# A recurrence in a two-block stack: 16x16 inversions of two units in one pass over 128 lanes, and the products of decayed queries, of removal keys and of the gate's additive part on GpSimd

## The chip, the cores and the metric

The kernel runs on one core of one Trainium2 chip. The metric is the device time of one execution in microseconds (us). The kernel before takes 2347.31 us, the median of 3 runs (2346.71 to 2354.41).

## What is computed

The kernel computes two transformer blocks of two layers each, one after the other, for 256 tokens of width 1024, and the second one also for 256 context tokens. Nearly all of its arithmetic is large projections. The change lies in one mixer, that of the second block's first layer, which runs an attention and beside it a recurrence over the 512 tokens, once forward and once backward, in 8 heads of 64:

```python
def wkv7_scan(S0, inputs, reverse):
    def step(S, inp):
        r, w, k, v, kk, a = inp
        S = (S * w[:, :, None, :]
             - jnp.einsum('bhvk,bhk->bhv', S, kk)[..., None] * (kk * a)[:, :, None, :]
             + v[..., None] * k[:, :, None, :])
        return S, jnp.einsum('bhvk,bhk->bhv', S, r)
    S, y = lax.scan(step, S0, xs, reverse=reverse)

def rwkv7_readout(y, feat, r_k, gn_w, gn_b):
    yn = ((y - mean) * lax.rsqrt(var + GN_EPS)).reshape(Bsz, T, B_WIDTH_2) * gn_w + gn_b
    bonus = (jnp.sum(r * k * r_k, axis=-1, keepdims=True) * v).reshape(Bsz, T, B_WIDTH_2)
    return ((yn + bonus.astype(jnp.float32)) * g.astype(jnp.float32)).astype(g.dtype)
```

The readout's gate is applied as G = gn_w g and H = (gn_b + bonus) g, so that the output is yn' G + H; H is the gate's additive part. The kernel doesn't step token by token: over a chunk of 64 tokens the recurrence becomes matrix products and the inverse of a triangular 64x64 matrix for each head, which is built from the inverses of its four 16x16 blocks on the diagonal.

## The kernel before, in words

The program is written with pools of named tiles; every engine (TensorE or PE, VectorE or DVE, ScalarE or ACT, GpSimd or POOL, and SyncE or SP, whose queue issues all the transfers that are spoken of here) has its own list of instructions. A scheduler puts the instructions of each engine in order, from the order in which the program issues them and from when their operands are ready, before the run; at run time each engine goes through its list and waits at the first instruction whose operands aren't there. A helper `tt` records the operations of two tensors on DVE (all at L120), `acopy` copies on ScalarE (L223) and `vcopy` on DVE (L226).

The work of the recurrence is cut into 8 **units**: a direction d (0 forward, 1 backward) and a tile t of 128 tokens, that is two chunks of 64. A unit passes these steps:

- **Front** (`rwkv_in` L1453, up to its first `yield`): the decays. sg goes through ScalarE (L1475), eo and ei hold the exponents of the summed decays and of their negatives, ak gets the rates.
- **Back** (the rest of `rwkv_in`): fe is loaded with r, k and kk (L1500; one buffer, so that the load waits for the unit before). DVE multiplies the keys, two products in ak, then the removal keys and the queries with the decays into ar (L1515 and L1516, `ar[:, :, 2]` and `ar[:, :, 1]`), then ak, and last bk, which is written over the first two thirds of fe (L1519). PE makes the matrices of each head (gg and gh, L1531) of ak and ar, DVE masks them into g. The triangular matrices go to dq in DRAM (L1543), for the backward direction after a transposition on DVE (L1541).
- **Solve** (`rwkv_solve` L1559): dl, loaded from dq (L1563), has one 16x16 block on each of 64 lanes: 2 chunks x 8 heads x 4 blocks. For 14 columns DVE makes a product dt and adds it to dl, 28 operations of 14 to 56 elements for each lane; the diagonal is set, and dy goes to DRAM (L1571).
- **Maps** (`rwkv_maps` L1573): the inverses come back as x (L1592), are transposed (L1593), and two rounds of `product` and `update` (32 matmuls m each, L1598) make the 64x64 inverses of them; between, am is built of ar and of v (L1626), and the products of x1 and am (L1640) go into lw; the products of g and lw (L1654) become z, which is stored over g.
- **Steps** (`rwkv_step` L1662): two for each pair of units, the chain of states si (L1672) and the outputs y (L1681) into yac.

`rwkv` (L1272) runs ten rounds: round n has the back of unit n, the front of unit n+2, the solve of unit n and the maps of unit n-2, and after each odd unit's maps two steps. Between the stages `fill` takes pieces of the attention (`gqa`, scores sc at L1010, transposes L1028, outputs po L1056, with K, vv and qS loaded from DRAM). After units 2 and 3 the gates (`gates` L1378: H = v x bonus + gn_b, then times g) and the readouts run as a side stream. Fronts, backs and solves of the first units come earlier, in `even_mixer` (L1078), in a written order with the last projections:

```python
GA = "l0 q0 r0 r1 r2 r3 k0 f0 v0 b0 s0 f1 f2 b1 f3 s1 v1 v2 v3"
```

(f, b and s are front, back and solve of a unit; v0 to v3 are the four blocks of v, each copied into the one buffer st, L1168, and from there stored to vd, L1170.) Six memsets of lw and si on GpSimd (L1280, L1284) begin `rwkv`; their tiles take the place of tiles of the projections.

Of the kernel before, what the change touches and what calls it, by code (L numbers as in the profile page):

```python
# [12 lines left out]
F32 = mybir.dt.float32  # L13
F32R = mybir.dt.float32r
AF = mybir.ActivationFunctionType
ALU = mybir.AluOpType
# [30 lines left out]
@with_exitstack  # L47
def kernel(ctx: ExitStack, tc: tile.TileContext, A: dict, out: bass.AP, taps=None):
    nc = tc.nc
    V, S, E = nc.vector, nc.scalar, nc.tensor  # L50
    taps = taps or {}

    cpool = ctx.enter_context(tc.tile_pool(name="cpool", bufs=1))
# [4 lines left out]
    def nm(s):  # L58
        uid[0] += 1
        return f"{s}_{uid[0]}"  # L60
# [13 lines left out]
    def pst(tag):  # L74
        pool, n = psum[tag]
        return pool.tile([128, 512], F32, tag=tag, name=nm(tag), bufs=n)
# [6 lines left out]
    def const(name, pool=cpool, tag=None, queue=nc.sync):  # L83
        src = A[name]
        t = pool.tile(list(src.shape), F32, tag=tag or name, name=nm(name))
        queue.dma_start(out=t, in_=src)
        return t
# [31 lines left out]
    def tt(o, a, b, op):  # L119
        V.tensor_tensor(out=o, in0=a, in1=b, op=op)  # L120
# [24 lines left out]
    def bc(ap, n):  # L145
        return ap.unsqueeze(2).to_broadcast([ap.shape[0], ap.shape[1], n])
# [931 lines left out]
    def even_mixer(l, en):  # L1078
        T = 512
        close_psum()  # L1080
        with tc.tile_pool(name=nm("em"), bufs=1) as pk, tc.tile_pool(name=nm("rf"), bufs=2) as fp, \
# [9 lines left out]
            C = {n: const(n, pk) for n in ("rwkv_wa", "rtri", "gmask", "tmask", "eye2", "sgn")}  # L1091
# [6 lines left out]
            bon = pk.tile([128, 4, 8], F32, tag="bon", name="bon")  # L1098
            order = []
            for i, (t0, t1) in enumerate(((2, 3), (0, 1))):  # L1100
                order += [dict(d=d, t=t, u=u, i=i) for u, (d, t) in enumerate(((0, t0), (1, t1), (0, t1), (1, t0)))]
            dq = [dp.tile([64, 1040], F32, tag=f"dq{n}", name=nm("dq")) for n in range(NS)]
            dy = [dp.tile([64, 1040], F32, tag=f"dy{n}", name=nm("dy")) for n in range(NS)]
# [20 lines left out]
            with tc.tile_pool(name=nm("emn"), bufs=1) as wk:  # L1124
# [4 lines left out]
                for j in range(2):  # L1129
                    z, f = en.tile("fu", 512), en.tile("fg", 512, 2)  # L1130
                    tt(z, pss[j], en.rb, ALU.mult)
                    for v in range(2):
                        c = slice(v * 256, v * 256 + 256)
# [12 lines left out]
            with tc.tile_pool(name=nm("ga"), bufs=1) as ga, tc.tile_pool(name=nm("emw"), bufs=2) as wk:  # L1146
# [72 lines left out]
                def do_r(f):  # L1219
# [21 lines left out]
                    for i, x in enumerate((rf, kf, kk)):  # L1241
                        nc.sync.dma_start(out=D["f"][:, 4 * i + f], in_=x)

                units = [rwkv_in(fp, C, D, un) for un in order]

                def front(u):
# [3 lines left out]
                    order[u].update(next(units[u]))  # L1250

                def solve(u):
                    rwkv_solve(C, order[u])

                def do_v(f):
                    vf = shifted(8 + f)
                    stage(D["v"][:, :, f * 128:(f + 1) * 128], 4, [vf[:, t * 128:(t + 1) * 128] for t in range(4)])

                do = dict(k=do_k, q=do_q, l=do_l, r=do_r, v=do_v, f=front, b=back, s=solve)
                for what, n in GA:  # L1260
                    do[what](n)
# [3 lines left out]
            close_half(0)  # L1265
            open_psum(gg=1, m=2, y=1, sc=1, tr=1)
            rwkv(C, D, order, (front, back, solve), bon, yac)
            for cm in reversed(held):
                cm.__exit__(None, None, None)
# [108 lines left out]
    def gates(D, bon, tm, t):  # L1378
        G, H = tm["G"], tm["H"]
        tok = slice(t % 2 * 128, t % 2 * 128 + 128)  # L1380
        nc.sync.dma_start(out=tm["gl"][:, tok], in_=D["lo"][:, 2, t * 128:(t + 1) * 128])
        nc.sync.dma_start(out=H, in_=D["v"][:, t])
        hg = H.rearrange("p (h d) -> p h d", h=8)
        tt(hg, hg, bc(bon[:, t], 64), ALU.mult)
        tt(H, H, tm["gn"][:, 512:], ALU.add)
        yield
        ps = pst("fr")
        E.matmul(out=ps, lhsT=tm["gl"][:, tok], rhs=tm["g2"], start=True, stop=True)
        tt(G, tm["gn"][:, :512], ps, ALU.mult)
        tt(H, H, ps, ALU.mult)  # L1390
        yield
        if t < 2:
            for i, x in enumerate((G, H)):
                nc.sync.dma_start(out=D["g"][:, 2 * t + i], in_=x)
# [55 lines left out]
    def half(i):  # L1450
        return slice(64 * i, 64 * i + 64)

    def rwkv_in(fp, C, D, un):  # L1453
        d, t, u, dq = (un[n] for n in ("d", "t", "u", "dq"))
# [4 lines left out]
        def w512(tag, shape=(128, 4, 128), pool=fp, bufs=None):  # L1459
            return pool.tile(list(shape), F32, tag=tag, name=nm(tag), **({"bufs": bufs} if bufs else {}))  # L1460
# [26 lines left out]
        inc, exc = eo[:, :, :, 1 - d:65 - d], eo[:, :, :, d:64 + d]  # L1487
# [10 lines left out]
        up, wk = C["up"][un["up"]], C["us"]  # L1498
        fe = w512("fe", (128, 12, 128), wk)
        nc.sync.dma_start(out=fe, in_=D["f"][:, :, tok])  # L1500
        rT, kT, kk = fe[:, 0:4], fe[:, 4:8], fe[:, 8:12]
        def c4(a):
            return a.rearrange("p f (c t) -> p f c t", c=2)

        def by_chunk(a):
            return a.rearrange("p f (c s) t -> p (f c) s t", c=2)
# [4 lines left out]
        ar = w512("ar", (128, 4, 3, 128), up)  # L1511
        for f in range(4):
            for ch in range(2):
                S.activation(out=ar[:, f, 0, ch * 64:ch * 64 + 64], in_=C["eye2"], func=AF.Copy, scale=pc[:, f, ch:ch + 1])
        tt(c4(ar[:, :, 2]), c4(kk), exc, ALU.mult)  # L1515
        tt(c4(ar[:, :, 1]), c4(rT), inc, ALU.mult)  # L1516
        tt(by_chunk(ak), by_chunk(ak), ei.rearrange("p f c t -> p (f c) t").unsqueeze(2).to_broadcast([128, 8, 2, 64]), ALU.mult)
        bk = fe[:, 0:8].rearrange("p n t -> p (n t)").rearrange("p (f a t) -> p f a t", f=4, a=4)
        tt(bk.rearrange("p f (c s) t -> p f c (s t)", c=2), ak.rearrange("p f (c s) t -> p f c (s t)", c=2),  # L1519
# [36 lines left out]
    def lanes_of(x):  # L1556
        return x[:, 0:1024].rearrange("l (r c) -> l r c", r=16)[:, :, 0:16]

    def rwkv_solve(C, un):  # L1559
        wk = C["us"]  # L1560

        y = wk.tile([64, 16, 16], F32, tag="dl", name=nm("dl"), bufs=2)
        nc.sync.dma_start(out=y, in_=lanes_of(un["dq"]))  # L1563
        for c in range(1, 15):
            n = 15 - c
            tmp = wk.tile([64, 64], F32, tag="dt", name=nm("dt"), bufs=2)
            o = tmp[:, :c * n].rearrange("p (a r) -> p a r", a=c)
            tt(o, y[:, 0:c, c].unsqueeze(2).to_broadcast([64, c, n]), y[:, c, c + 1:16].unsqueeze(1).to_broadcast([64, c, n]), ALU.mult)
            tt(y[:, 0:c, c + 1:16], y[:, 0:c, c + 1:16], o, ALU.add)
        V.memset(y.rearrange("p a r -> p (a r)")[:, 0:256:17], 1.0)  # L1570
        nc.sync.dma_start(out=lanes_of(un["dy"]), in_=y)  # L1571

    def rwkv_maps(C, D, un):  # L1573
        d, t, u, dy, ar, g = (un[n] for n in ("d", "t", "u", "dy", "ar", "g"))
# [213 lines left out]
    with tc.tile_pool(name="fin", bufs=1) as wk:  # L1788
# [3 lines left out]
        for k in range(0, 8, 2):  # L1792
            o = en.tile("fo", 512, 4).rearrange("p (k t) -> p k t", k=2)
# [133 lines left out]
def _build(arrays, taps=()):  # L1927
    import concourse.bacc as bacc

    nc = bacc.Bacc("TRN2", target_bir_lowering=False, num_devices=1)  # L1930
    A = {n: nc.dram_tensor(f"in_{n}", a.shape, mybir.dt.from_np(a.dtype), kind="ExternalInput").ap() for n, a in arrays.items()}
    out = nc.dram_tensor("out_0", (128, 8, 256), F32, kind="ExternalOutput").ap()
    tp = {n: (nc.dram_tensor(f"tap_{n}", s, F32, kind="ExternalOutput").ap() if s else None) for n, s in dict(taps).items()}
    with tile.TileContext(nc) as tc:
        kernel(tc, A, out, tp)
    return nc
# [10 lines left out]
```

## Time and profile before

| what | value |
|---|---|
| median of 3 runs | 2347.31 us |
| the profiled execution | 2347.3 us, span 2345.5 us |
| busy PE | 2242.3 us, 96% |
| busy DVE | 1568.0 us, 67% |
| busy ACT | 1072.6 us, 46% |
| busy POOL | 5.6 us, 0% |
| granted PE clock, mean | 0.982 |

The profile is of one execution. The span is the time from the first to the last recorded instruction; busy times are sums over an engine's instructions and overlap between engines. The granted clock is the share of PE's full clock that the chip allowed. In the timelines a bracket tells how long the engine was idle before the instruction and what released it.

### The profile page before, as it was taken

Reading aid. Unit: us, or ns where it says so; the run is one execution under the profiler, and the core shown is the slowest. Engines: PE = TensorE matmul, PEld = TensorE weight load, DVE = VectorE, ACT = ScalarE, POOL = GpSimd, SP = SyncE. Lnnn points to the kernel's source line nnn. Section 1 sums busy time; section 2 is a strip of 40 time slices with the busy share of each in tenths; the row PEclk is TensorE's granted clock in tenths of the full one; section 3 lists DMA queues with packets and bytes.
Section 4 is the critical chain, followed back from the end, with each engine's and each line's share of the span. In section 5 each row is a group of like instructions: output and inputs, shape, how many; then the busy total and the mean of one; then the engine's idle time right before and its main releaser. Section 6 shows DMA issues by size and latency. Waiting matters only on the chain.

```text
span 2345.5 us, 35440 instructions
## 1 busy us (share of the span) xinstructions
PE 2242.3 (96%) x13642; PEld 1835.2 (78%) x13642; DVE 1568.0 (67%) x3074; ACT 1072.6 (46%) x1884; POOL 5.6 (0%) x10
## 2 busy tenths in 40 slices
PE   8999998999999998998888999999999999989998
PEld 6688787777787786776667788787778788768998
DVE  7867778766845677889587777338654334786555
ACT  6756666312224637765545222235322223476444
POOL 0000000000000000000000000000000000000000
PEclk9999999999999999999999999999999999999999
DMA  8556545555623545533264565323543232314553
GB/s 293 175 184 212 173 149 165 194 165 167 198 89 115 157 147 138 123 87 83 76 207 135 181 195 182 103 88 132 189 162 132 87 98 97 99 33 140 182 184 121
DMA packets 161946, 342.02 MB, mean 146 GB/s; under 512 B 48625, under 2 KB 76273, under 8 KB 161649
## 3 DMA queue, kind: packets, MB, share of 16 engines
q1 hardware_dynamic: 161056, 339.15, 45.6%
q8 instruction: 108, 1.77, 0.3%
q10 hardware_dynamic: 720, 0.60, 0.1%
q14 instruction: 62, 0.50, 0.1%
HBM read 321.86 MB, written 17.84 MB: 145 GB/s over the span
## 4 chain that ended last, share of the span: by engine, by line
PE 87%; DVE 7%; ACT 4%; DMA 1%; issue 1%; SPq 0%; DVEq 0%; ACTq 0%
PE mm L115 25%; PE mm L117 24%; PE mm L116 24%; PE m L1598 1%; DVE wlo L98 1%; PE tr L219 1%; PE m L1654 1%; DMA fe<-fd 1%; ACT whi L97 1%; PE wm L331 1%; PE po L1056 1%; PE wm L274 1%; PE gg L1531 1%; PE po L541 1%; DVE xl L129 0%
## 5 line engine op out<-in xcount | busy, mean ns | idle before, releaser
L97 ACT CAST whi<-raw 128x1024 fp32r<-128x1024 f32 (+2 forms) x437 | 437.3, 1002 | 984.6 <-PE mm L116 591.5
L115 PE MATMUL mm<-xh,whi 128*128 128x512 f32 (+1 forms) x1912 | 680.1, 359 | 16.6 <-ACT xh L97 9.5
L117 PE MATMUL mm<-xh,wlo 128*128 128x512 f32 (+1 forms) x1912 | 678.1, 356 | 5.2 <-DVE wlo L98 5.0
L116 PE MATMUL mm<-xl,whi 128*128 128x512 f32 (+1 forms) x1912 | 678.6, 356 | 1.2 <-DVE xl L98 1.1
L98 DVE TENSOR_TENSOR wlo<-raw,whi 128x1024 fp32r<-128x1024 f32 (+2 forms) x437 | 507.6, 1163 | 257.2 <-ACT whi L97 251.2
L115 PEld LDWEIGHTS mm<-xh,whi 128*128 128x128 f32 x1912 | 364.5, 191 | 81.1 <-ACT whi L97 16.1
L117 PEld LDWEIGHTS mm<-xh,wlo 128*128 128x128 f32 x1912 | 364.4, 191 | 58.0 <-DVE wlo L98 7.3
L116 PEld LDWEIGHTS mm<-xl,whi 128*128 128x128 f32 x1912 | 364.8, 191 | 53.8 <-DVE xl L98 4.2
L117 PE MATMUL mm<-hh,wlo 128*128 128x512 f32 (+1 forms) x704 | 260.1, 370 | 0.0
L116 PE MATMUL mm<-hl,whi 128*128 128x512 f32 (+1 forms) x704 | 257.9, 366 | 0.1
L115 PE MATMUL mm<-hh,whi 128*128 128x512 f32 (+1 forms) x704 | 257.0, 366 | 0.0
L129 DVE SCALAR_TENSOR_TENSOR macc<-raw,modc,macc 128x1024 f32<-128x1024 f32 x189 | 234.4, 1279 | 0.5
L129 DVE SCALAR_TENSOR_TENSOR xres<-mm,mod,xres 128x256 f32<-128x256 f32 x216 | 96.3, 480 | 164.2 <-PE mm L117 163.9
L120 DVE TENSOR_TENSOR fg<-mm,fg 128x512 f32<-128x512 f32 (+1 forms) x84 | 52.4, 624 | 161.3 <-PE mm L117 160.6
L115 PEld LDWEIGHTS mm<-hh,whi 128*128 128x128 f32 x704 | 132.1, 188 | 27.6 <-issue 2.5
L116 PEld LDWEIGHTS mm<-hl,whi 128*128 128x128 f32 x704 | 132.4, 188 | 26.1 <-DVE hl L98 0.7
L115 PE MATMUL mm<-whi,xh 128*128 128x512 f32 (+1 forms) x360 | 143.4, 404 | 9.2 <-ACT whi L97 8.5
L117 PEld LDWEIGHTS mm<-hh,wlo 128*128 128x128 f32 x704 | 132.2, 188 | 22.9
L116 PE MATMUL mm<-wlo,xh 128*128 128x512 f32 (+1 forms) x360 | 143.7, 399 | 2.8 <-DVE wlo L98 2.8
L117 PE MATMUL mm<-whi,xl 128*128 128x512 f32 (+1 forms) x360 | 142.2, 397 | 0.0
L115 PEld LDWEIGHTS mm<-whi,xh 128*128 128x128 f32 x360 | 68.5, 191 | 31.3 <-ACT whi L97 9.8
L116 PEld LDWEIGHTS mm<-wlo,xh 128*128 128x128 f32 x360 | 69.0, 192 | 17.3 <-DVE wlo L98 5.3
(402 smaller groups left out, 2524.0 us busy)
## 6 DMA issues: line engine op xcount, KB each, us to landing
raw<-in_ffn_in SPq DMA_DIRECT2D x176, 512.0 KB, 3.5
raw<-in_w_mod SPq DMA_DIRECT2D x144, 512.0 KB, 4.5
raw<-in_ffn_out SPq DMA_DIRECT2D x64, 448.0 KB, 3.3
raw<-in_w_in_even SPq DMA_DIRECT2D x32, 512.0 KB, 4.8
raw<-in_w_in_odd SPq DMA_DIRECT2D x32, 512.0 KB, 3.7
raw<-in_ffn_out SPq DMA_DIRECT2D x32, 512.0 KB, 3.5
raw<-in_w_ple_gate SPq DMA_DIRECT2D x16, 512.0 KB, 3.6
raw<-in_even_r SPq DMA_DIRECT2D x15, 512.0 KB, 3.5
```

The costliest lines, as they stand in the source:

```text
L97: S.copy(out=hi, in_=src)
L98: V.tensor_tensor(out=lo, in0=src, in1=r32(hi), op=ALU.subtract)
L115: E.matmul(out=ps, lhsT=ah, rhs=bh, start=first, stop=False)
L116: E.matmul(out=ps, lhsT=ah, rhs=bl, start=False, stop=False)
L117: E.matmul(out=ps, lhsT=al, rhs=bh, start=False, stop=last)
L120: V.tensor_tensor(out=o, in0=a, in1=b, op=op)
L129: V.scalar_tensor_tensor(out=o, in0=a, scalar=s, in1=b, op0=op0, op1=op1)
L219: E.transpose(ps[:, j * 128:(j + 1) * 128], s, ident)
L274: E.matmul(out=ps[32 * j:32 * j + 32, hf * 256:hf * 256 + 256], lhsT=cz[:, 4 * g + j, 10 - 2 * c:42 - 2 * c], rhs=raw[:, j], start=c == 0 ...
L331: E.matmul(out=ps[32 * j:32 * j + 32], lhsT=mod_1[:, 2 - q:34 - q], rhs=acc[:, v, hf * 512:hf * 512 + 512], start=q == 0, stop=q == 2)
L541: E.matmul(out=po[:, 0:128], lhsT=pt[:, j * 128:(j + 1) * 128], rhs=vt[:, j, c], start=j == 0, stop=j == nk - 1)
L1056: E.matmul(out=po[half(a), 0:256], lhsT=vt[:, j], rhs=pt[:, j, 2 * a:2 * a + 2], start=j == 0, stop=j == nk - 1)
```

## The change

Three edits. `rwkv_solve` takes two units: dl has 128 lanes, unit n-1 on the first 64 and unit n on the others, with two loads and two stores, and the 28 operations work on both at once; `solve(u)` does nothing for an even u, and for an odd one solves u-1 and u together, so that s0 in the written order is empty and s1 is the solve of both. In the backs, the two products into ar are issued by GpSimd in place of DVE. In the gates, the two operations that make H before the matmul (times bon, plus gn_b) are too. Line numbers after L1250 rise by 1, after L1571 by 3.

```diff
@@ even_mixer
                 def solve(u):
-                    rwkv_solve(C, order[u])
+                    if u % 2:
+                        rwkv_solve(C, order[u - 1], order[u])
@@ gates
         hg = H.rearrange("p (h d) -> p h d", h=8)
-        tt(hg, hg, bc(bon[:, t], 64), ALU.mult)
-        tt(H, H, tm["gn"][:, 512:], ALU.add)
+        P.tensor_tensor(out=hg, in0=hg, in1=bc(bon[:, t], 64), op=ALU.mult)
+        P.tensor_tensor(out=H, in0=H, in1=tm["gn"][:, 512:], op=ALU.add)
@@ rwkv_in
-        tt(c4(ar[:, :, 2]), c4(kk), exc, ALU.mult)
-        tt(c4(ar[:, :, 1]), c4(rT), inc, ALU.mult)
+        P.tensor_tensor(out=c4(ar[:, :, 2]), in0=c4(kk), in1=exc, op=ALU.mult)
+        P.tensor_tensor(out=c4(ar[:, :, 1]), in0=c4(rT), in1=inc, op=ALU.mult)
@@ rwkv_solve
-    def rwkv_solve(C, un):
+    def rwkv_solve(C, *uns):
-        y = wk.tile([64, 16, 16], F32, tag="dl", name=nm("dl"), bufs=2)
-        nc.sync.dma_start(out=y, in_=lanes_of(un["dq"]))
+        y = wk.tile([128, 16, 16], F32, tag="dl", name=nm("dl"), bufs=2)
+        for i, un in enumerate(uns):
+            nc.sync.dma_start(out=y[half(i)], in_=lanes_of(un["dq"]))
...
-            tmp = wk.tile([64, 64], F32, tag="dt", name=nm("dt"), bufs=2)
+            tmp = wk.tile([128, 64], F32, tag="dt", name=nm("dt"), bufs=2)
...
-        nc.sync.dma_start(out=lanes_of(un["dy"]), in_=y)
+        for i, un in enumerate(uns):
+            nc.sync.dma_start(out=lanes_of(un["dy"]), in_=y[half(i)])
```

The order of GpSimd's instructions, from its first one in the recurrence on, of the kernel before (lw and si are the tiles of the maps and the steps; the last row is a branch at the program's end):

```order
L1280 MEMSET lw_9057 128x1024
L1280 MEMSET lw_9058 128x1024
L1280 MEMSET lw_9061 128x1024
L1280 MEMSET lw_9062 128x1024
L1284 MEMSET si_9065 128x1024
L1284 MEMSET si_9071 128x1024
L1934 UNCONDITIONAL_BRANCH
```

And of the change, up to unit 3's products (the first two pairs are units 0 and 1, the two after the memsets units 2 and 3):

```order
L1516 ISA
L1516 TENSOR_TENSOR ar_8609<-fe_8605,eo_8542 128x4x128
L1517 TENSOR_TENSOR ar_8609<-fe_8605,eo_8542 128x4x128
L1516 TENSOR_TENSOR ar_8735<-fe_8731,eo_8676 128x4x128
L1517 TENSOR_TENSOR ar_8735<-fe_8731,eo_8676 128x4x128
L1281 MEMSET lw_9013 128x1024
L1281 MEMSET lw_9014 128x1024
L1281 MEMSET lw_9017 128x1024
L1281 MEMSET lw_9018 128x1024
L1285 MEMSET si_9021 128x1024
L1285 MEMSET si_9027 128x1024
L1516 TENSOR_TENSOR ar_9054<-fe_9050,eo_8711 128x4x128
```

The six memsets stand between unit 1's products and unit 2's.

SP's queue at the handover from the projections to the recurrence, before (dl loads and dy stores are the inversions', vd the blocks of v, vv, K and qS the attention's):

```order
L1563 DMA dl_8870<-dq_7252 64x16x16
L1500 DMA fe_9094<-fd 128x12x128
L1571 DMA dy_7255<-dl_8661 64x16x16
L1170 DMA vd<-st_8994 512x1x128
L1439 DMA qS_9138<-qd 128x512
L1439 DMA qS_9140<-qd 128x512
L1592 DMA x_2010_9281<-dy_7255 64x8x64
L1170 DMA vd<-st_9037 512x1x128
```

The same place in the change:

```order
L1565 DMA dl_8824<-dq_7252 64x16x16
L1501 DMA fe_9050<-fd 128x12x128
L1430 DMA vv_9090<-vvd 128x512
L1438 DMA K_9092<-kd 128x1024
L1170 DMA vd<-st_8993 512x1x128
L1440 DMA qS_9094<-qd 128x512
L1440 DMA qS_9096<-qd 128x512
L1473 DMA sg_9473<-in_rwkv_w 128x512
L1374 DMA ro_9042<-in_gn 128x1024
L1375 DMA ro_9043<-in_rwkv_g 128x512
L1580 DMA lw_9013<-vd 64x4x128
L1574 DMA dy_7255<-dl_8824 64x16x16
```

The dy of unit 0, ahead of v's third block (vd<-st_8994) before, stands behind v's fourth (vd<-st_8993 in the change) now, with that of unit 1 right behind it.

PE's order in the last unit's maps, before (sc, tr and gp are attention, m the maps, y the steps of the pair before and of the last one):

```order
L1598 MATMUL m_11760<-x_2424_11754,g_11065 64x64 x16
L1056 MATMUL tr_11820<-gpt_11614,vv_9134 64x256
L1672 MATMUL y_11922<-si_9065,g_10706 64x64 x8
L1010 MATMUL sc_11971<-K_10833,qS_11609 128x256 x2
L1028 MATMUL tr_11979<-ident_63,gp_11965 128x128
L1598 MATMUL m_11778<-x_2425_11755,T_2426_11759 64x64 x16
L1028 MATMUL tr_11979<-ident_63,gp_11965 128x128
L1010 MATMUL sc_12021<-K_10833,qS_11609 128x256 x2
L1028 MATMUL tr_12029<-ident_63,gp_11972 128x128 x2
L1010 MATMUL sc_12033<-K_10833,qS_11609 128x256
L1598 MATMUL m_11803<-x_2424_11754,g_11065 64x64 x16
```

And in the change:

```order
L1056 MATMUL tr_11874<-gpt_11787,vv_9090 64x256 x3
L1657 MATMUL m_11550<-g_10574,lw_9014 128x128 x4
L1675 MATMUL y_11746<-si_9021,g_10574 64x64
L1657 MATMUL m_11557<-g_10574,lw_9014 128x128 x4
L1675 MATMUL y_11746<-si_9021,g_10574 64x64 x7
L1601 MATMUL m_11584<-x_2364_11578,g_10887 64x64 x16
L1601 MATMUL m_11602<-x_2365_11579,T_2366_11583 64x64 x16
L1601 MATMUL m_11627<-x_2364_11578,g_10887 64x64 x16
L1629 MATMUL m_11654<-ident_63,ar_10874 128x128 x4
```

The last attention outputs stand ahead of unit 6's last map now, and no attention lies between the products of unit 7.

## Rows read from the trace of the kernel before

**Rows 1.** The page, part 1: busy us, share of the span, instructions.

```profile
PE 2242.3 (96%) x13642; PEld 1835.2 (78%) x13642; DVE 1568.0 (67%) x3074; ACT 1072.6 (46%) x1884; POOL 5.6 (0%) x10
```

**Rows 2.** Stretches of the recurrence: us, busy us by engine (instructions), clock, DMA share, GB/s.

```profile
930.00:950.00 20.00, 11.57 (x76) 8.14 (x76) 16.45 (x56) 12.51 (x35) 5.39 (x6) 0.66 0.79 191
...
950.00:1060.00 110.00, 104.87 (x1460) 85.30 (x1458) 93.06 (x258) 79.03 (x192) 0.00 (x0) 1.00 0.40 97
...
1060.00:1125.00 65.00, 54.53 (x796) 43.72 (x796) 60.48 (x163) 34.08 (x62) 0.00 (x0) 1.00 0.35 89
...
1160.00:1175.90 15.90, 6.61 (x110) 5.94 (x110) 9.81 (x18) 5.90 (x12) 0.00 (x0) 0.57 0.37 111
```

**Rows 3.** Timeline of the handover: start us, us, engine, line, operation, count, [idle <-releaser].

```profile
931.98 0.59 SPq L1571 DMA_DIRECT2D dy<-dl  x1
...
932.33 0.63 ACT L1475 ACTIVATE sg<-sg 128x512 f32<-128x512 f32 x1
...
932.62 1.20 SPq L1170 DMA_DIRECT2D vd<-st  x1
...
937.05 0.58 ACT L223 COPY st<-tr 128x512 f32<-128x512 f32 x1 [4.09 <-DMA vd<-st]
...
937.78 1.19 PE L1010 MATMUL sc<-K,qS 128*128 128x512 f32 x2 [3.20 <-ACT st L223]
...
944.04 0.58 PE L1531 MATMUL gg<-ar,ak 64*128 64x128 f32 x1 [1.20 <-DVE ar L120]
```

**Rows 4.** Timeline of PE, units 5 to 7, 1100 to 1173 us.

```profile
1107.03 1.96 PE L1640 MATMUL m<-am,x 64*64 64x128 f32 x32
...
1119.72 1.15 PE L1681 MATMUL y<-si,g 128*64 128x64 f32 x32 [1.38 <-ACT si L223]
...
1131.36 1.96 PE L1640 MATMUL m<-am,x 64*64 64x128 f32 x32 [0.23 <-DVE x L120]
...
1151.38 1.96 PE L1640 MATMUL m<-am,x 64*64 64x128 f32 x32 [0.51 <-DVE x L120]
...
1157.03 2.17 PE L1654 MATMUL m<-g,lw 128*128 128x128 f32 x16
...
1170.31 1.98 PE L1681 MATMUL y<-si,g 128*64 128x64 f32 x32 [1.39 <-ACT si L223]
```

**Rows 5.** Tile dl: duration ns min/median/max, first and last start, forms.

```profile
L120 DVE TENSOR_TENSOR dt<-dl x112: 125/189/212, 915.8 to 1122.6; 64x14 f32<-64x14 f32 x16, 64x26 f32<-64x26 f32 x16, 64x36 f32<-64x36 f32 x16, 64x44 f32<-64x44 f32 x16
```

**Rows 6.** Timeline of DVE, units 6 and 7, 1087 to 1133 us.

```profile
1087.99 0.20 DVE L120 TENSOR_TENSOR dt<-dl 64x56 f32<-64x56 f32 x1
...
1088.12 0.68 DVE L120 TENSOR_TENSOR ro<-ro,ro 128x512 f32<-128x512 f32 x1
...
1105.96 0.68 DVE L120 TENSOR_TENSOR x<-x,m 128x512 f32<-128x512 f32 x1
...
1123.02 0.17 DVE L120 TENSOR_TENSOR dl<-dl,dt 64x14 f32<-64x14 f32 x1
...
1131.79 0.70 DVE L1593 STREAM_TRANSPOSE x<-x 128x512 f32<-128x512 f32 x1
```

**Rows 7.** Tiles ar and ro on DVE: duration ns min/median/max.

```profile
L120 DVE TENSOR_TENSOR ar<-fe,eo x16: 664/677/691, 896.1 to 1081.4; 128x512 f32<-128x512 f32 x16
...
L120 DVE TENSOR_TENSOR ro<-ro,bon x4: 676/692/693, 965.8 to 1116.8; 128x512 f32<-128x512 f32 x4
```

**Rows 8.** Groups on GpSimd: count, busy us, mean ns, idle before.

```profile
L1280 POOL MEMSET lw<- 128x1024 f32 x4 | 3.6, 952 | 940.2 <-DVE dl L120 940.2
...
L1284 POOL MEMSET si<- 128x1024 f32 x2 | 1.8, 952 | 0.0
```

**Rows 9.** Timeline of DVE, unit 7's maps.

```profile
1145.48 0.70 DVE L1619 STREAM_TRANSPOSE x<-x 128x512 f32<-128x512 f32 x1
...
1147.78 0.69 DVE L120 TENSOR_TENSOR T<-m,tmask 128x512 f32<-128x512 f32 x1 [1.23 <-PE m L1598]
...
1150.55 0.69 DVE L120 TENSOR_TENSOR x<-x,m 128x512 f32<-128x512 f32 x1 [0.28 <-PE m L1598]
```

More of the change, by code (lines that the diff above doesn't have):

```diff
@@ L49 @@
     nc = tc.nc
-    V, S, E = nc.vector, nc.scalar, nc.tensor
+    V, S, E, P = nc.vector, nc.scalar, nc.tensor, nc.gpsimd
     taps = taps or {}
@@ L1557, in lanes_of @@
         return x[:, 0:1024].rearrange("l (r c) -> l r c", r=16)[:, :, 0:16]
-    def rwkv_solve(C, un):
+    def rwkv_solve(C, *uns):
         wk = C["us"]
-        y = wk.tile([64, 16, 16], F32, tag="dl", name=nm("dl"), bufs=2)
-        nc.sync.dma_start(out=y, in_=lanes_of(un["dq"]))
+        y = wk.tile([128, 16, 16], F32, tag="dl", name=nm("dl"), bufs=2)
+        for i, un in enumerate(uns):
+            nc.sync.dma_start(out=y[half(i)], in_=lanes_of(un["dq"]))
         for c in range(1, 15):
             n = 15 - c
-            tmp = wk.tile([64, 64], F32, tag="dt", name=nm("dt"), bufs=2)
+            tmp = wk.tile([128, 64], F32, tag="dt", name=nm("dt"), bufs=2)
             o = tmp[:, :c * n].rearrange("p (a r) -> p a r", a=c)
-            tt(o, y[:, 0:c, c].unsqueeze(2).to_broadcast([64, c, n]), y[:, c, c + 1:16].unsqueeze(1).to_broadcast([64, c, n]), ALU.mult)
+            tt(o, y[:, 0:c, c].unsqueeze(2).to_broadcast([128, c, n]), y[:, c, c + 1:16].unsqueeze(1).to_broadcast([128, c, n]), ALU.mult)
             tt(y[:, 0:c, c + 1:16], y[:, 0:c, c + 1:16], o, ALU.add)
         V.memset(y.rearrange("p a r -> p (a r)")[:, 0:256:17], 1.0)
-        nc.sync.dma_start(out=lanes_of(un["dy"]), in_=y)
+        for i, un in enumerate(uns):
+            nc.sync.dma_start(out=lanes_of(un["dy"]), in_=y[half(i)])
     def rwkv_maps(C, D, un):
```

## The prediction

> **What bounds the kernel now.** I read the page first: TensorE (PE) is busy for 96% of the span [rows 1], so a change that takes nothing off PE can at best remove some of the 103 us in which PE is not busy (2345.5 less 2242.3). The profiled execution took 2347.3 us around a span of 2345.5, and the median of the runs is 2347.31, so a shift of the span is a shift of the median. Then I cut the recurrence, 885 to 1176 us, into stretches [rows 2]. In 930 to 950, the handover from the projections to the recurrence, PE is busy 11.57 of 20 us and its granted clock is 0.66: part of the time at the lower of its two levels (1.2 against 2.4 GHz), after PE had stood still. In 950 to 1060 PE misses 5.1 us of 110, in 1060 to 1125 it misses 10.5 of 65 while VectorE (DVE) is busy 60.48, and in 1160 to 1175.9 it is busy 6.61 of 15.9 at a clock of 0.57. So the reader is to see three places: a handover that waits, a middle where DVE is as full as PE, and a tail in which one unit's chain runs alone.
>
> Who ends the handover's gap stands in the timeline [rows 3]. SP's queue issues dy of unit 0 at 931.98, when DVE has ended its solve; only then, 932.62, the copy of v's third block. That lands before ScalarE can copy the next block at 937.05 (4.09 us idle, released by that DMA), and PE's first attention matmul waits 3.20 us for this copy. Each unit's maps then follow each other on PE: the products with am (L1640) of units 5, 6 and 7 start at 1107.03, 1131.36 and 1151.38, and the last step ends at 1170.31 + 1.98 = 1172.3 [rows 4].
>
> **The change part by part.**
>
> *Inversions.* Before, 112 multiplies of 0.19 us [rows 5] and, one behind each, as many adds: 28 operations to a unit. 128 lanes take the place of 64 with the same free sizes, so I keep 0.19 for each and 4 x 28 go: 21 us of busy time. Placed between larger operations one takes less of DVE's time: 1087.99 to 1088.12, 0.13 us [rows 6]; so 15 to 21 us. The price is time of waiting: unit 6 now waits until unit 7 is ready, and SP's dy of both stand where dy of the later one stood.
>
> *Products to GpSimd.* 16 operations of 0.68 us leave DVE, and 8 of 0.68 to 0.69 in the gates [rows 6, 7]: 16 us. The trace shows GpSimd only in memsets: 952 ns for 1024 columns [rows 8], 0.48 us for one pass over 512. Two reads and a write, as three such passes, give 1.43 us. Bounds: 0.48 (one pass) and, above, twice my value, 2.9, as a memset says nothing of arithmetic. I take 1.43, the row being GpSimd's own. A new wait comes with it: DVE's product that overwrites fe (L1519) must wait until GpSimd has read fe. In a unit's front DVE still has 0.6 + 0.6 + 1.2 us before it, against 2 x 1.43 = 2.9: a wait of 0.5, behind which stand softmax and map operations; before, the two products held DVE for 1.2 there. Net 0.7 us less for each unit at my price; at 2.9, 3.4 - 1.2 = 2.2 more. The gates have slack (their vd load is waited for only by themselves), so they cost nothing as long as attention fills PE; uncovered, 2.9 us for a token block.
>
> *GpSimd's queue.* Unit 2's products stand behind the six memsets, 5.7 us [rows 8], which themselves wait for the end of the projections' buffers (before: released at 940.2). Before, PE waited for ar of unit 2 until 944.04 [rows 3]. Now 940.2 - 2 (the handover, below) + 5.7 + 2.9 = 946.8, so 2.8 us later, partly under attention that PE has in front of it; I take 1.
>
> *Handover.* SP now issues v's third and fourth blocks ahead of both dy. The third no longer waits for DVE; the fourth still waits for ScalarE, which has the fronts' work and sg in front of it. Before, sg ended there at 932.96 [rows 3]; I take 932.5 for the fourth block's copy, then issues of 0.6 us for vd and two qS and, an estimate from the 8.6 us that a store, a load and a transpose take below, some 2.5 to land: PE's attention near 936.3 in place of 937.78, 1.5 us. With the memsets' 1 us: **-0.5 us**, range -4 to +2.
>
> *Middle.* By 1107 DVE has lost 3 pairs' worth of inversions and nearly all 16 products, 25 to 30 us, but PE misses there only 5.1 us and, of the 10.5 in 1060 to 1125, some 8 by the length of that stretch that lies before 1107 (47 of 65). A gap ends with whatever is late next: ScalarE's exponents and lw copies, or fe. I take nearly half: **-6 us**, range 0 to -13 (13 is all that PE misses there).
>
> *Unit 5 to unit 6.* Before, 24.3 us between their L1640 [rows 4]. Now unit 6's x comes from the joint inversion of units 6 and 7, and this begins, in DVE's order, only 5 inversion operations ahead of unit 5's last x add. From that add to the end of unit 7's inversion before, 1105.96 to 1123.19, were 17.2 us [rows 6]; without four gate products and a map product of unit 6 (about 3.7) 13.5. The way from there to x in place was 1123.19 to 1131.79 = 8.6 [rows 6]: store, load, transpose. Then come four rounds of product, DVE, with 1.15 us of PE (32 passes, as the y products' in rows 4) and 0.69 of DVE and two short handshakes (2.05 each), and two transposes of 0.70 [rows 4, 9]: 9.6. Minus 1.1 from add to L1640: 30.6, **+6.3 us**. Range +3 to +9.
>
> *Unit 6 to unit 7.* Before 20.0 us with attention between. Now attention is used up before unit 7, its x is there early, and maps run bare: from L1640 to the end of the last map matmul 7.8 (1151.38 to 1159.20) [rows 4], then 4 x 2.05 + 0.7 = 8.9: 16.7, **-3.3 us**.
>
> *Tail.* From unit 7's L1640 to the end 20.9 as before. But a bare unit keeps PE busy about half the time; in 1160 to 1175.9 such a share went with a granted clock of 0.57, and the same 32 passes of y took 1.98 us in place of 1.15 [rows 4]. Unit 7's maps hold some 11 us of PE; if a third to a half of it runs at the lower level, **+3 us**, range 0 to +8.
>
> *Sum:* -0.5 - 6 + 6.3 - 3.3 + 3 = -0.5 us against 2347.3: **2346.8 us**, which is within 0.3% (7 us), about what a measurement of this kernel can tell from no change. Ends of the terms that go together (good handover, full relief; or none and a cold tail) give -11 and +10.
>
> Here rows and a rule differ. While the memsets ran, from 940.2 on, DVE worked on, unit 2's products among its operations, and of all 16 none took over 0.691 us [rows 7, 8]: GpSimd beside it cost DVE nothing. The Trainium skill, SBUF — State Buffer, section "Who interferes with whom", says that a DVE instruction with two SBUF inputs contends with a GpSimd instruction that reads SBUF, not with one that only writes; by that rule the memsets show nothing and the moved products would hold DVE up. No run here shows it yet; it is the third rival, and the sum without it stands.
>
> **The rivals.**
>
> *DVE is the bound throughout.* For it: 60.48 of 65 us busy in 1060 to 1125. Against: in 950 to 1060, with DVE at 85%, PE missed only 5%. If all 13 us before 1107 go and the handover gives 4: -4 - 13 + 6.3 - 3.3 + 3 = -11, **2336 us**.
>
> *The bare tail runs at the lower clock; slower.* From unit 6's first product on attention is nearly used up, so PE has the maps of two units, some 11 us each (four products of 1.15, 2.0 for L1640, about twice that for L1654), at 1.98/1.15 of their time: 2 x 7.9 = 15.8 in place of the 3 in the sum: **2360 us**. It decides if the granted clock has fallen before unit 6's L1640; that the clock stayed at 1.00 while PE was busy 54.53 of 65 us speaks against it, that it fell in both stretches with less speaks for it [rows 2].
>
> *Shared reads.* DVE and GpSimd take turns: a front's 2.4 us of DVE and 2.9 of GpSimd stand one behind the other, 5.3 against 3.6 before bk, 1.7 more where the sum has 0.7 less. Eight units: 19 us of DVE time, of which the middle gives on a fifth, as above, and the last two fronts all: 3 + 5, about +8: **2355 us**.
>
> *GpSimd late.* An operation of 2.9 us, or a first one that takes long, makes DVE's fe product wait 3.4 us and PE's gg with it, in each unit: 8 x 2.2 = 18, of which two thirds show where PE has little else: **2359 us**.
>
> **How the numbers follow.** Forecast 0.47 (2341 to 2352); DVE the bound 0.24; cold tail 0.11; shared reads 0.12; GpSimd late 0.06. Faster by over 0.3%: the first rival and a little of the forecast, 0.25. Slower: cold tail, GpSimd late and a third of shared reads, with a little of the forecast, 0.22. Within: 0.53. The range for 8 in 10 leaves out the far sides of the first and the slow cases: 2334 to 2359.
>
> **What would show it.** In the changed profile: PE's first attention matmul near 936 (handover); moved products on GpSimd of 1.4 us, and DVE's L120 operations beside them no longer than before (shared reads else); L1643 (then) of units 5, 6, 7 near 1100, 1131 and 1147; the granted clock in the 40 us before the last step above 0.8; last step near 1171. The forecast is wrong if the three gaps shrink together by over 10 us, or if unit 6's x is in place later than 1125.

## The result, and the profile after

The changed kernel takes 2375.69 us (median of 4 runs, 2374.36 to 2377.88) against 2350.76 for the kernel before in the same comparison (4 runs, 2346.71 to 2354.41): a ratio of 1.0107, 95% interval 1.0083 to 1.0132, that is 25 us slower. The forecast was 2346.8, the range ended at 2359. The runs of the kernel before spread over some 14 us in all comparisons (2345.6 to 2360.0), and its profiled execution, 2347.3, lies at the fast end; so the ratios below carry the verdicts, and the profiles show places.

Part 1 of the page of the changed kernel:

```profile
span 2372.2 us, 35351 instructions
...
PE 2257.5 (95%) x13642; PEld 1843.9 (78%) x13642; DVE 1558.0 (66%) x2934; ACT 1072.9 (45%) x1884; POOL 36.7 (2%) x34
```

Against [rows 1], DVE has 140 instructions fewer, as it should have (112 + 24, and 4 memsets of a joined dl), but only 10 us less busy time. The forecast counted 15 to 21 us for the inversions and 16 for the products. PE has the same 13642 instructions and is busy 15.2 us longer with them; it is idle 114.7 us (2372.2 less 2257.5) in place of 103.2. So less than half of the loss, 11.5 us, is visible as waiting; the rest is the same work taking longer, with a lower granted clock in part of it. The stretches of [rows 2], with the same columns, the last one now 1184 to 1198.5:

```profile
930.00:950.00 20.00, 10.67 (x41) 6.99 (x42) 13.54 (x43) 13.34 (x38) 7.70 (x8) 0.66 0.77 213
950.00:1060.00 110.00, 98.62 (x1350) 79.52 (x1350) 81.14 (x167) 70.23 (x167) 13.33 (x10) 0.98 0.36 88
1060.00:1125.00 65.00, 57.01 (x739) 45.58 (x739) 54.09 (x119) 35.42 (x67) 7.45 (x6) 0.89 0.29 70
...
1184.00:1198.50 14.50, 5.42 (x115) 4.59 (x113) 7.04 (x15) 2.75 (x5) 0.00 (x0) 0.79 0.17 51
```

DVE did become emptier, in 950 to 1060 from 93.06 to 81.14 and in the next stretch from 60.48 to 54.09, but PE did not become fuller: 110 fewer matmuls in the first of the two, 57 fewer in the second, and a clock that now falls there to 0.98 and 0.89 from 1.00.

Where the time went is read from one instruction group of each unit, the products with am; only these lines are taken out of the timelines. Timeline of PE, the kernel before, units 0 to 4 (units 5 to 7 are in [rows 4]):

```profile
962.48 1.96 PE L1640 MATMUL m<-am,x 64*64 64x128 f32 x32
989.39 1.96 PE L1640 MATMUL m<-am,x 64*64 64x128 f32 x32 [1.86 <-DVE dl L120]
1019.41 1.96 PE L1640 MATMUL m<-am,x 64*64 64x128 f32 x32
1046.72 1.96 PE L1640 MATMUL m<-am,x 64*64 64x128 f32 x32
1074.00 1.20 PE L1640 MATMUL m<-am,x 64*64 64x128 f32 x18 [0.88 <-DVE x L120]
```

The same in the changed kernel, units 0 to 7:

```profile
968.75 1.49 PE L1643 MATMUL m<-am,x 64*64 64x128 f32 x23 [2.21 <-DVE eo L1481]
996.44 1.96 PE L1643 MATMUL m<-am,x 64*64 64x128 f32 x32
1031.50 3.25 PE L1643 MATMUL m<-am,x 64*64 64x128 f32 x32
1056.46 1.96 PE L1643 MATMUL m<-am,x 64*64 64x128 f32 x32
1096.26 1.96 PE L1643 MATMUL m<-am,x 64*64 64x128 f32 x32
1121.32 1.96 PE L1643 MATMUL m<-am,x 64*64 64x128 f32 x32 [0.29 <-DVE dl L120]
1157.21 1.96 PE L1643 MATMUL m<-am,x 64*64 64x128 f32 x32
1176.41 1.96 PE L1643 MATMUL m<-am,x 64*64 64x128 f32 x32 [1.38 <-DVE x L120]
```

| from | to | before | after | difference |
|---|---|---|---|---|
| start | unit 0 | 962.5 | 968.8 | +6.3 |
| unit 1 | unit 2 | 30.0 | 35.1 | +5.0 |
| unit 3 | unit 4 | 27.3 | 39.8 | +12.5 |
| unit 5 | unit 6 | 24.3 | 35.9 | +11.6 |
| inside the four pairs, sum | | 107.3 | 96.9 | -10.4 |
| unit 7 | last step's end | 20.9 | 18.4 | -2.5 |
| last step's end | end of span | 1173.2 | 1177.4 | +4.2 |

The differences add up to the 27 us between the spans. Every step from a pair to the next is longer, and part of it comes back inside the pairs, whose second unit now has its x soon after the first. The +6.3 at the start says little by itself: in the profiled executions of runs 9 and 11 below, which cost nothing (ratios 1.0001 and 1.0005), unit 0's product stands at 969.27 and 972.79. The last row has no instruction of the change in it: from 1200 to 1300 the granted clock is 0.88, and 0.95 before.

The handover, as far as it answers to [rows 3], in single lines from the timeline of the changed kernel:

```profile
935.24 0.58 ACT L223 COPY st<-tr 128x512 f32<-128x512 f32 x1 [2.17 <-PE tr L219]
935.85 0.56 SPq L1170 DMA_DIRECT2D vd<-st  x1
940.81 1.19 PE L1010 MATMUL sc<-K,qS 128*128 128x512 f32 x2 [4.75 <-DMA sg<-in_rwkv_w]
943.57 1.32 SPq L1574 DMA_DIRECT2D dy<-dl  x2
946.67 0.58 PE L1532 MATMUL gg<-ar,ak 64*128 64x128 f32 x1 [0.80 <-POOL ar L1517]
953.25 0.70 DVE L1596 STREAM_TRANSPOSE x<-x 128x512 f32<-128x512 f32 x1
```

The copy of v's fourth block no longer waits for DVE's solve, as expected. It now waits for PE's transposition of the block and starts at 935.24, not at 932.5, and attention begins at 940.81, where a DMA ends PE's wait. The gg of unit 2, behind the memsets, was put at 946.8 and stands at 946.67. And the dy of unit 0 goes out at 943.57 with that of unit 1, 11.6 us later than before, so that its x is transposed at 953.25; before, at 944.01:

```profile
944.01 0.70 DVE L1593 STREAM_TRANSPOSE x<-x 128x512 f32<-128x512 f32 x1
```

On GpSimd the groups stand so (mean ns behind the comma):

```profile
L1517 POOL TENSOR_TENSOR ar<-fe,eo 128x512 f32<-128x512 f32 x8 | 11.3, 1415 | 0.0
L1516 POOL TENSOR_TENSOR ar<-fe,eo 128x512 f32<-128x512 f32 x8 | 10.0, 1245 | 1038.6 <-ACT eo L1486 911.5 <-DMA fe<-fd 105.0 <-DVE dl L120 22.1
L1386 POOL TENSOR_TENSOR ro<-ro,ro 128x512 f32<-128x512 f32 x4 | 6.0, 1498 | 0.3
```

The price of 1.43 us for one was met, but by luck: the product at 895.59, beside which no DVE operation with two inputs in SBUF ran, took 1.18 us, and others took up to 1.7 beside DVE's products with fe. What it does to DVE was priced at nothing. The timeline of DVE, from unit 5's last x addition to unit 6's x; before, the inversion's dt operations took 0.13 to 0.21 [rows 5]:

```profile
1120.48 0.69 DVE L120 TENSOR_TENSOR x<-x,m 128x512 f32<-128x512 f32 x1 [0.24 <-PE m L1601]
...
1122.30 0.98 DVE L120 TENSOR_TENSOR dl<-dl,dt 128x50 f32<-128x50 f32 x1
1123.32 1.32 DVE L120 TENSOR_TENSOR dt<-dl 128x54 f32<-128x54 f32 x1
...
1131.29 1.27 DVE L124 TENSOR_SCALAR gp<-gp,s 128x512 f32<-128x512 f32 x1
1132.48 1.26 DVE L120 TENSOR_TENSOR dt<-dl 128x36 f32<-128x36 f32 x1
...
1136.88 0.17 DVE L120 TENSOR_TENSOR dl<-dl,dt 128x14 f32<-128x14 f32 x1
...
1145.22 0.71 DVE L1596 STREAM_TRANSPOSE x<-x 128x512 f32<-128x512 f32 x1
```

The four long ones lie beside the gates' operations on GpSimd, which run from 1122.2 to 1124.6 and from 1131.2 to 1133.7. Operations that take 0.2 us or 0.48 elsewhere last about as long here as GpSimd's own instruction.

### The profile page after: what moved, and what is told of

Read it like the earlier page. It is cut to its first block, busy times and chain, and to the rows that moved or that the text cites. A ratio compares the mean times of both kernels' runs of the same rounds, so it can differ in the third digit from the quotient of the medians.

```text
span 2372.2 us, 35351 instructions
## 1 busy us (share of the span) xinstructions
PE 2257.5 (95%) x13642; PEld 1843.9 (78%) x13642; DVE 1558.0 (66%) x2934; ACT 1072.9 (45%) x1884; POOL 36.7 (2%) x34
## 4 chain that ended last, share of the span: by engine, by line
PE 87%; DVE 7%; ACT 3%; issue 1%; DMA 1%; POOL 0%; SPq 0%; DVEq 0%; ACTq 0%
PE mm L115 25%; PE mm L117 24%; PE mm L116 24%; PE m L1601 1%; PE m L1657 1%; PE tr L219 1%; DVE wlo L98 1%; DVE ak L120 1%; PE wm L274 1%; PE wm L331 1%; PE po L1056 1%; ACT whi L97 1%; PE po L541 1%; PE m L1643 1%; PE tr L1056 0%
## 5 line engine op out<-in xcount | busy, mean ns | idle before, releaser
L115 PE MATMUL mm<-xh,whi 128*128 128x512 f32 (+1 forms) x1912 | 680.8, 359 | 16.3 <-ACT xh L97 9.4
```

Source lines behind the costliest of these rows:

```text
L115: E.matmul(out=ps, lhsT=ah, rhs=bh, start=first, stop=False)
```

## The experiments

Two theories were set against each other. **Partner**: the first unit of a pair waits for the second one's back and then for the joint inversion. **Shared reads**: DVE is held while GpSimd reads. Ratios are against the kernel before of the same comparison; 0.1% is 2.35 us.

**1 and 2. Each half alone.** Against the changed kernel, the first run puts the four kinds of operations back on DVE (the two of the backs are shown, the two of the gates left out here), the second undoes the joined inversions (the call is shown):

```diff
-        P.tensor_tensor(out=c4(ar[:, :, 2]), in0=c4(kk), in1=exc, op=ALU.mult)
-        P.tensor_tensor(out=c4(ar[:, :, 1]), in0=c4(rT), in1=inc, op=ALU.mult)
+        tt(c4(ar[:, :, 2]), c4(kk), exc, ALU.mult)
+        tt(c4(ar[:, :, 1]), c4(rT), inc, ALU.mult)
```

```diff
-                    if u % 2:
-                        rwkv_solve(C, order[u - 1], order[u])
+                    rwkv_solve(C, order[u])
```

> All products back on DVE, only the inversions of two units at once are kept. Partner theory (the first unit of a pair waits for the back of the second and then for the joint inversion): most of the loss stays, 2365 to 2378 us, and the gaps between the L1643 products of units 1 and 2, 3 and 4, 5 and 6 stay near 35, 40 and 36 us. Shared-read theory (GpSimd's products hold DVE up): 2340 to 2352 us.

> The kernel before with the products of the backs and of the gates on GpSimd, inversions one unit at a time. Partner theory: 2343 to 2354 us, the gaps between the units' products with am as before. Shared-read theory: 2358 to 2375 us, with DVE operations of 1.2 us that take about 2 us beside GpSimd.

Joined inversions alone: 2371.01 us, 1.0081 (1.0066 to 1.0097). Products on GpSimd alone: 2372.53 us, 1.0090 (1.0073 to 1.0106). Neither theory has it all: each half costs 19 to 21 us by itself. Together they cost 25, so a part of the two losses is the same time. Run 1's time is the partner theory's, but of its three gaps only the last is: 28.9 us from unit 1 to 2 (before 30.0), 33.1 from 3 to 4 and 37.6 from 5 to 6. Unit 0's product stands at 978.76 there, 16.3 us later than before, and behind so late a start the next pair has less to wait for: with the middle pairs alone joined (run 5) unit 0 is only 0.9 us late and the step from unit 1 to 2 takes 34.2 us.

**3 to 5. Which pairs.** Inversions joined for some pairs only, products on DVE:

```diff
-                    if u % 2:
-                        rwkv_solve(C, order[u - 1], order[u])
+                    if u < 2:
+                        if u % 2:
+                            rwkv_solve(C, order[u - 1], order[u])
+                    else:
+                        rwkv_solve(C, order[u])
```

with `u < 2`, `u < 6` and `2 <= u < 6`.

> Inversions joined for units 0 and 1 alone, products on DVE. Partner theory: each joined pair costs its own boundary; this pair's is the handover, which was 6.3 us later at unit 0's product with am in the changed kernel: 2350 to 2357 us. A theory in which the whole loss comes from the changed order of SP's queue at the handover would give 2365 us or more.

> Inversions joined for the first three pairs, units 6 and 7 apart, products on DVE. Partner theory: the boundary from unit 5 to unit 6 goes back to about 24 us from 36, so about 11 us less than with all four pairs joined: 2355 to 2367 us. If the tail were what matters less and the middle pairs cost nothing, 2347 to 2352 us.

> Inversions joined for units 2 and 3 and for 4 and 5 alone, products on DVE. From the runs before, joining the first pair cost some 9 us and the last some 11, and three pairs together no more than the first alone. If a joined pair costs only where PE has no other work in front, these two cost nothing: 2344 to 2355 us, within 3 us of the kernel before or below it. If every pair costs by itself: 2358 us or more.

The first pair alone: 2358.78 us, 1.0029 (1.0015 to 1.0042), 7 us, 1.8 us above what the partner theory gave. The first three: 2357.42 us, 1.0026 (1.0016 to 1.0037), 6 us. The two middle ones: 2356.94 us, 1.0029 (1.0013 to 1.0044), 7 us, between the two answers that were set for it. So the last pair makes 13 of the 19 us, and the other three together no more than one of them. In the timeline of PE the last boundary is 37.6 us with all pairs joined and 24.0 with the last two units apart. First all four pairs joined, units 0, 5 and 6:

```profile
978.76 1.96 PE L1643 MATMUL m<-am,x 64*64 64x128 f32 x32
...
1117.89 1.96 PE L1643 MATMUL m<-am,x 64*64 64x128 f32 x32
1155.53 1.96 PE L1643 MATMUL m<-am,x 64*64 64x128 f32 x32 [0.51 <-DVE x L120]
```

Then the last pair apart, units 5 and 6:

```profile
1117.87 1.96 PE L1647 MATMUL m<-am,x 64*64 64x128 f32 x32
1141.90 1.96 PE L1647 MATMUL m<-am,x 64*64 64x128 f32 x32 [0.23 <-DVE x L120]
```

At unit 5 the two executions are 0.02 us apart, and at no unit before it more than 0.42. Of the 13.8 us between their spans (2370.0 and 2356.2), 13.6 arise between unit 5 and unit 6, with no GpSimd operation of the change in either.

**6 and 7. Which products.** The kernel before with the gates' eight operations on GpSimd, and with the backs' sixteen (the lines of the diff of run 1, the other way round, one kind at a time):

> Only the eight operations of the gates on GpSimd. Shared-read theory: each holds DVE for about 1 us, eight of them 8 us of DVE time, of which part shows: 2350 to 2360 us. Theory that only the backs' products do harm, since PE waits for ar and DVE for fe: 2345 to 2353 us.

> Only the sixteen products of the backs on GpSimd. Theory that only these do harm: nearly the whole of the 19 us of both kinds together, 2364 to 2374 us. Theory that it is shared reads alone, whatever the operation: two thirds of it, 2360 to 2366 us.

Gates: 2352.42 us, 1.0011 (0.9999 to 1.0022), which both answers allow. Backs: 2369.77 us, 1.0087 (1.0073 to 1.0101), nearly all of what both cost. The gates' operations hold DVE too: its busy time is 1571.1 us with 8 instructions of 0.69 fewer than the 1568.0 of [rows 1], 8.6 us more than it should be. Of that hold at most 0.22%, some 5 us, can show in the time, by the interval.

**8 and 9. Hold without a wait for the result.** All products stay on DVE; GpSimd computes one of them twice more into a tile that nobody reads. In run 9 each of these has 8 columns in place of 512:

```diff
         tt(c4(ar[:, :, 1]), c4(rT), inc, ALU.mult)
+        sc = w512("scr", pool=wk, bufs=1)
+        for i in range(2):
+            P.tensor_tensor(out=c4(sc), in0=c4(kk), in1=exc, op=ALU.mult)
```

> The kernel before with all products on DVE, and in each back GpSimd computes the removal keys' product twice more into a tile that nobody reads (work is added, none is left out): GpSimd's reads without anyone waiting for its results. Shared-read theory: DVE operations beside these sixteen get about 1 us longer each, 2355 to 2372 us. Theory that the harm comes from waiting for GpSimd's results (ar late behind the memsets, fe held): 2344 to 2353 us.

> As the run with the removal keys' product twice more on GpSimd, but each of the sixteen added products has 8 columns in place of 512: same instructions, same dependences, GpSimd busy for a small part of the time. Shared-read theory: the hold lasts as long as GpSimd's instruction, so most of the 18 us go: 2349 to 2357 us, and no DVE operation of 0.2 us takes 1.1. Theory that it is the order and the waits that the added instructions bring: 2363 us or more, as before.

Full length: 2368.58 us, 1.0083 (1.0068 to 1.0098). Eight columns: 2355.13 us, 1.0001 (0.9988 to 1.0015). By the ratios, the same instructions with the same dependences cost 19.5 us or nothing, by their length alone; and they cost as much as the moved products did, though nobody waits for what they compute. Nor is it the order: on DVE, ScalarE and SP's queue it is the same in both runs as in the kernel before, and on PE too, but for a few neighbours that start together. In run 8's profile no wait of any engine is put down to the added products. Run 8's page has DVE with the 3074 instructions of the kernel before and 13.5 us more busy time, 0.84 us for each added product:

```profile
PE 2259.9 (95%) x13642; PEld 1849.4 (78%) x13642; DVE 1581.5 (67%) x3074; ACT 1073.1 (45%) x1884; POOL 32.0 (1%) x26
```

How it gets to PE is seen in unit 5's back. Full length, timeline of DVE, POOL and PE:

```profile
1032.07 2.28 DVE L120 TENSOR_TENSOR ak<-ak,fe 128x512 f32<-128x512 f32 x2 [1.78 <-DMA fe<-fd]
1032.21 3.18 POOL L1519 TENSOR_TENSOR scr<-fe,eo 128x512 f32<-128x512 f32 x2 [33.23 <-DMA fe<-fd]
1034.27 1.14 DVE L120 TENSOR_TENSOR dt<-dl 64x14 f32<-64x14 f32 x1
...
1038.00 0.37 PE L1534 MATMUL gg<-ar,ak 64*128 64x128 f32 x1 [2.33 <-DVE ak L120]
```

Eight columns:

```profile
1027.01 1.30 DVE L120 TENSOR_TENSOR ak<-ak,fe 128x512 f32<-128x512 f32 x2 [1.86 <-DMA fe<-fd]
1027.15 1.22 POOL L1519 TENSOR_TENSOR scr<-fe,eo 128x8 f32<-128x8 f32 x2 [32.99 <-DMA fe<-fd]
1028.23 0.16 DVE L120 TENSOR_TENSOR dt<-dl 64x14 f32<-64x14 f32 x1
...
1030.98 0.37 PE L1534 MATMUL gg<-ar,ak 64*128 64x128 f32 x1 [0.46 <-DVE ak L120]
```

From DVE's first product with fe to the first gg, 5.93 us against 3.97: the two products with fe take 1.0 longer, the small dt another 1.0, and PE waits 2.33 in place of 0.46. fe lands, DVE and GpSimd start on it within 0.14 us, and DVE's chain from there to gg is what PE waits for. The other units are not all like this one. From unit 0 to 7 the stretch is longer by 0.3, 1.1, 1.9, 0.0, 3.1, 2.0, 0.9 and 2.7 us, 11.9 in all, and the two spans are 11.8 apart (2368.2 and 2356.4). But PE's own wait ahead of the first gg is longer in units 1 and 5 only; by which waits the rest reaches PE is not shown.

**10 and 11. The partner earlier.** The program issues both backs of a pair in the even round, ahead of the joint inversion, and the fronts of the next pair with them; run 11 has the same order and the inversions apart:

```diff
-                        for do, what in zip((back, front, solve), "bfs"):
-                            u = n + 2 * (what == "f")
-                            if u < 8 and (what, u) not in GA:
+                        for do, what, u in ((back, "b", n), (front, "f", n + 2), (back, "b", n + 1), (front, "f", n + 3), (solve, "s", n), (solve, "s", n + 1)):
+                            if n % 2 == 0 and u < 8 and (what, u) not in GA:
                                 do(u)
```

> All inversions joined, products on DVE, and the program issues the backs of both units of a pair (and the fronts of the next pair) one round earlier for the second unit, right ahead of their joint inversion; the first pair is as it was. Partner theory: the waits of the last pair (some 11 us) and of the middle ones (some 4) shrink or go, the first pair's 9 us stay: 2355 to 2363 us against 2371 for the joined inversions in the old order. If the length of the joint inversion itself on DVE is the cause: 2368 us or more.

> The kernel before with the backs and fronts issued by pairs as in the run with joined inversions, inversions one unit at a time: the control for the order alone. Partner theory: the order alone changes little, 2346 to 2358 us; if it costs or gives more than that, the run with joined inversions has to be read against this one.

Joined: 2364.78 us, 1.0043 (1.0027 to 1.0058). Apart: 2355.01 us, 1.0005 (0.9990 to 1.0020). The kernel before stood at 2354.26 in this comparison, so the median is 2 us outside what the partner theory gave, while the ratio is half of run 1's 1.0081. The order alone costs nothing; with it, 9 of the 19 us of joining go. What is left stands elsewhere: unit 0's product comes at 990.25, 17.5 us later than in run 11, and the step from unit 3 to 4 takes 36.2 us (run 11: 27.6). The last boundary is 26.5 us (units 5 and 6 of run 10):

```profile
1125.78 2.86 PE L1642 MATMUL m<-am,x 64*64 64x128 f32 x32 [0.15 <-DVE dl L120]
1152.31 1.97 PE L1642 MATMUL m<-am,x 64*64 64x128 f32 x32
```

**12. Relief alone.** Every second column of the inversions is left out, 112 operations of DVE:

```diff
-        for c in range(1, 15):
+        for c in range(1, 15, 2):
```

> The kernel before with every second of the inversion's 14 columns left out for each unit (so this leaves work out: 7 multiplies and 7 additions in each of the 8 units, 112 operations of DVE, as many as the joined inversions save). It relieves DVE without a new wait, and each unit's inverse is ready earlier by the same operations. If DVE bounds the recurrence, as the prediction's term of the middle had it in part: 6 us or more off, 2335 to 2345 us. If the relief is worth nothing there: 2347 to 2355 us.

2352.13 us, 1.0003 (0.9994 to 1.0012). DVE's busy time falls by 13.9 us, and nothing comes of it:

```profile
PE 2252.9 (96%) x13642; PEld 1844.1 (78%) x13642; DVE 1554.1 (66%) x2962; ACT 1073.2 (46%) x1884; POOL 5.6 (0%) x10
```

No version of the change that these runs point to beats the kernel before: the relief from the inversions is worth nothing, so a joined pair can hardly do better than come out even. That the same holds for the products' relief is argued, not shown: no run takes them off DVE without the hold.

## Why the prediction was wrong

Two steps failed, each worth some 20 us by itself. The prediction's own signs of it came: unit 6's x is in place at 1145.22, where anything later than 1125 was to mean that the forecast is wrong, and DVE's operations beside the moved products are longer than before.

**"GpSimd beside it cost DVE nothing."** The step weighed the memsets of [rows 8], beside which DVE's products kept their 0.691 us, against the rule of the Trainium skill (SBUF — State Buffer, "Who interferes with whom"), and gave shared reads a chance of 0.12. The memsets have no tile to read, so the row could not speak on reads; runs 8 and 9 measure it. The trace agrees with the rule: DVE operations with two inputs in SBUF went from 0.16 to 1.14 us beside GpSimd's products. The rival's mechanism was right and its size was not: "a front's 2.4 us of DVE and 2.9 of GpSimd stand one behind the other" was put at 1.7 us longer for a unit, and run 8 against run 9 gives 1.5 on average; but that "the middle gives on a fifth" of it was wrong. The held operations are among the first ones behind the load of fe, on the chain to gg, and the 13.5 us of added DVE time in run 8 cost 19.5 us. The rival's +8 us for the products became some 20 in run 7.

**The handover and the middle: the first unit's wait was priced at one boundary of four.** The text saw that "unit 6 now waits until unit 7 is ready", and put it at +6.3 us from unit 5 to 6. The handover was summed from v's blocks and the memsets alone, and the middle held only relief. Unit 0 waits for unit 1 as well (x at 953.25 in place of 944.01), and the boundaries from 1 to 2 and from 3 to 4 grew by 5.0 and 12.5 (in run 1, without the hold, by -1.1 and 5.8 behind the later start). Runs 3 to 5 give 6 to 7 us for the first pair, for the middle two, or for these three together, in place of -0.5 and -6. The sum for the start of attention was also off in itself: 932.5, three issues of 0.6 and 2.5 make 936.8 and not 936.3.

**Unit 5 to unit 6**, mechanism right, size off: 11.6 us, and 13 by runs 1 and 4, in place of 6.3 with a range to 9. Of its terms, the way from the inversion's end to the transposed x held: 8.3 us (1136.88 to 1145.22) for 8.6. From unit 5's last x addition to that end it took 16.4 in place of 13.5, with the four held operations in it, some 3.7 us longer than alone. But the hold is not what the sum missed: in run 1, with the gates' products back on DVE, the same stretch also takes 16.4 (1116.64 to 1133.07). Why it is longer than 13.5 stays open. From the transposition to L1643 it took 12.0 in place of 9.6, with pieces of attention between the products on PE.

**The middle, -6 us**, and with it the rival of DVE as the bound: run 12 takes as many operations off DVE and leaves the time as it was (1.0003). An engine that is busy 60.48 of 65 us, and that another waits for now and then, need not be the bound. The -10.4 us inside the pairs need not be relief either: the second unit's x comes soon after the first one's, which was late.

**Bare maps at the tail**: from unit 6 to unit 7 19.2 us, where 16.7 was expected: 8.7 to unit 7's first product in place of 7.8, and 10.5 from there in place of 8.9. The +3 for a cold tail was wrong in sign: PE's last stretch took 18.4 us, the granted clock was 0.97 in the last 40 us before the last step's end, and the y products took 1.15 us until the very last:

```profile
1190.31 1.15 PE L1675 MATMUL y<-si,g 128*64 128x64 f32 x32 [1.58 <-DVE yac L120]
1192.85 1.98 PE L1684 MATMUL y<-si,g 128*64 128x64 f32 x32 [1.39 <-ACT si L223]
```

The rival with a low clock fails with it; the clock fell earlier, around the start of unit 4's maps:

```profile
1075.00:1095.00 20.00, 15.88 (x223) 13.34 (x222) 15.26 (x30) 6.42 (x11) 2.83 (x2) 0.66 0.36 84
```

**GpSimd late** (0.06): ar came late only for unit 2, as priced (946.67). Run 8, where nobody waits for GpSimd's results, costs as much as run 7.

What stays open: why the losses of the pairs, and those of the two halves, add up to less than their sum (6, 7 and 7 us; 19 and 21 against 25). For the pairs, runs 1 and 5 suggest that a late start shortens the waits behind it; no run tries it.

## What to carry to other kernels

Before moving an operation to GpSimd, ask which VectorE operations will run in the same moment, and whether they read two tensors from SBUF. Two engines that start on the same freshly loaded tile can collide in nearly every iteration (here in seven of eight units), on the chain that the next engine waits for. Joining two small serial jobs halves their instructions, but makes the first wait for the second; in a pipeline that wait can be paid at every hand-on, so price all of them, the first and last above all. Before trusting a busy engine's relief, leave work out of it once: if the time stays, there is nothing to win by that relief.

## What was not expected of the hardware

- In proportion the hold strikes small operations hardest: in run 8 DVE operations of the inversions, 0.16 to 0.20 us elsewhere, took 1.13 to 1.18 beside a GpSimd product, and in the changed kernel one on a single SBUF tensor with a scalar for each partition took 1.27 in place of 0.48. DVE operations with one input in PSUM kept their time there (T from m and the mask, 0.69, 0.58 of it beside GpSimd at 1025.81 in the changed kernel), as did reductions and transpositions (0.65 and 0.71 beside GpSimd at 964.4 to 965.7 in run 8). GpSimd's product is longer in turn: 1.18 us at its shortest and 1.65 on average in run 8.
- A GpSimd product of 8 columns lasts 0.20 us at its shortest in run 9 and 0.73 on average, as it is longer beside DVE's products with two inputs (0.70 beside one of 0.69 at 896.74). It holds nobody measurably: the small dt beside it took 0.16.
- More than half of the loss showed as longer busy time of PE for the same instructions, 15.2 of 26.7 us. And the kernel's own spread may have one of its places at the handover: run 9, whose ratio is 1.0001, had the lower of the two levels from 950 to 960 in its profiled execution (first line), where the profiled execution of the kernel before (second line) had the upper one; the columns are PE's busy time, granted clock, DMA share and GB/s:

```profile
950.00:960.00 10.00, 10.00 (x62) 0.50 0.48 132
```

```profile
950.00:960.00 10.00, 9.01 (x148) 1.00 0.90 208
```
